# FoX attention without the division by the weights' sum, with the meta block evicted beside the first full block

## The chip, the cores and the metric

One program on one core of a Trainium2 chip. The core has five engines with an in-order queue each: TensorE (PE: matrix products; its weight loads are shown as PEld), VectorE (DVE), ScalarE (ACT), GpSimd (POOL) and SyncE (SP), which starts most transfers. They wait for each other through semaphores. The metric is the time on the device in microseconds (us), the median of several runs.

## The reference

One layer of an encoder trunk over 16 meta tokens and 1024 positions (1040 rows, width 1024), in float32. After a normalisation one projection feeds three mixers: causal pooling, six heads of FoX (softmax attention with a cumulative forget gate as a bias) and six heads of stick-breaking attention. Each head's output is normalised over its 64 channels; an output projection, a gated feed-forward part and a last normalisation follow. What the change touches:

```
def head_rmsnorm(y, gain, n_heads):
    y32 = y.reshape(b, l, n_heads, HEAD_DIM)
    y32 = y32 * lax.rsqrt(jnp.mean(y32 * y32, axis=-1, keepdims=True) + EPS)
    return y32 * gain
...
s = jnp.einsum('bhqd,bhkd->bhqk', qb, k32) * scale
s = s + cb[..., None] - c[:, :, None, :]
s = jnp.where(pos[None, :] <= tq[:, None], s, -jnp.inf)
p = jax.nn.softmax(s, axis=-1)
o = jnp.einsum('bhqk,bhkd->bhqd', p, v)
```

The softmax divides each row by its sum l. With o' = l o the output before that division, o / sqrt(mean(o^2) + EPS) equals o' / sqrt(mean(o'^2) + EPS l^2): the division can be left out if EPS l^2 takes the place of EPS in the head norm.

## The kernel before

Products in full precision are made of halves: a float32 tile is rounded to the PE's format (the high half, ending in h: wh, ph, sh) and the rest (the low half, ending in l) is kept beside it; two or three products replace one. ACT or POOL make the high half (hi_pool is POOL's rounding, L77), DVE or POOL subtract for the low half.

Six pairs of heads go through attention: the first is stick-breaking, then three FoX pairs, then two stick-breaking pairs. The generator `attention` takes, for each pair, blocks of 256 queries (t from 3 to 0) of each head h: `fox_scores` or `sb_scores` make the weights P, a tile of 128 queries by the keys for each half block ii; `weighted`, one block later, turns them (a transpose is a PE product with the identity, L517 and L531), evicts the turned blocks from PSUM as ph (ACT, L520 and L538) and pl (DVE, L521 and L539), three tiles of each in turn, and multiplies them with the values (L511). The meta keys are block 0 with a tile of its own of 256 columns; of the last block of keys only the second half of the queries has weights, so that its pieces are 256 and 128 columns wide. `head_out` adds the two halves of the result (L398, L399). When both heads of a group of 512 queries are done, `head_norm` squares (L404), rounds (L77), subtracts (L408), takes the mean over a head's channels on PE by the matrix hmean (L410, L411), and makes the factor by a logarithm and an exponential on ACT (L413, L414); L415 applies it.

In `fox_scores` DVE adds the bias and finds the maximum (L495), ACT takes the exponential and the sum in one pass (L500), DVE inverts the sum (L501) and multiplies the weights by it (L502):

```
S.activation(P[:, :nk], P[:, :nk], AF.Exp, bias=st[:, 0:1], accum_out=st[:, 1:2])
V.reciprocal(st[:, 2:3], st[:, 1:2])
V.tensor_scalar(P[:, :nk], P[:, :nk], st[:, 2:3], None, ALU.mult)
```

A second generator, the filler, brings work for PE beside attention: the projections of the next pair (L289, with weights split on POOL, L77 and L164), the pooling mixers' pieces (L597 on, mostly DVE additions, L627 to L652), and at the end the output projection (L701). `interleave` writes the two in an order set by estimated costs; a scheduler then orders each engine's queue by a simulated timeline, so that the order of instructions is fixed when the program is built. The feed-forward part (L890, L1075) follows.

Of the kernel before, what the change touches and what calls it, by code (L numbers as in the profile page):

```python
# [17 lines left out]
NM = 16  # L18
# [12 lines left out]
def hymba_trunk(  # L31
# [59 lines left out]
    def mm(tag, shape, bufs):  # L91
        return T(ps, shape, F32, tag, bufs)
# [12 lines left out]
            T(at, [128, 512], F32, tag, n)  # L105


    ident = cst.tile([128, 128], F32, name="ident")
    make_identity(nc, ident)
    identb = cst.tile([128, 128], BF16, name="identb")  # L110
    V.tensor_copy(identb, ident)
    n1 = cst.tile([128, KD], F32, name="n1")
# [285 lines left out]
        S.copy(t[a:a + 64, :n], po[b:b + 64, :])  # L398
        V.tensor_tensor(op[a:a + 64, :], po[a:a + 64, :], t[a:a + 64, :n], ALU.add)  # L399

    def head_norm(op, gi, yt, last=False):
# [8 lines left out]
        PE.matmul(pm, hmean, sh, start=True, stop=False)  # L410
        PE.matmul(pm, hmean, sl, start=False, stop=True)  # L411
        f = T(at, [128, 512], F32, "nt", 2)
        S.activation(f, pm, AF.Ln, bias=epst[:, 0:1])  # L413
# [72 lines left out]

    def fox_scores(pr, h, t, cb):
        pr.pt = []
        for ii in range(2):
# [8 lines left out]
            st = T(ap_, [128, 3], F32, "fs", 4)  # L498
            V.tensor_scalar(st[:, 0:1], mx[:, len(pcs) - 1:len(pcs)], -1.0, None, ALU.mult)
            S.activation(P[:, :nk], P[:, :nk], AF.Exp, bias=st[:, 0:1], accum_out=st[:, 1:2])  # L500
            V.reciprocal(st[:, 2:3], st[:, 1:2])  # L501
            V.tensor_scalar(P[:, :nk], P[:, :nk], st[:, 2:3], None, ALU.mult)  # L502
            pr.pt.append(P)
            yield 1.2 * nk / 512

    def weighted(pr, h, t, ptiles, po):
        nkb = 2 * t + 3

        def av(kb, xs, c, first):
            for ix, x in enumerate(xs):  # L510
                PE.matmul(po[:, c:256], pr.v[h][:, kb, :], x, start=first and ix == 0,  # L511
                          stop=(kb == nkb - 1 and ix == 1), skip_group_check=True)


        tp = mm("s", [128, 512], SB_)
        for ii in range(2):
            PE.transpose(tp[:, 128 * ii:128 * ii + 128], ptiles[ii][:, 0:128], ident)  # L517
        ph = T(ap_, [128, 512], F32R, "ph", 3)
        pl = T(ap_, [128, 512], F32R, "pl", 3)
        S.copy(ph[:, :256], tp[:, :256])  # L520
        V.tensor_tensor(pl[:, :256], tp[:, :256], ph[:, :256], ALU.subtract)  # L521
        av(0, (ph[:, :256], pl[:, :256]), 0, True)
        kbs = list(range(1, nkb))
        for g in range(0, len(kbs), 2):
            pair = kbs[g:g + 2]
            tp = mm("s", [128, 2, 2, 128], SB_)
            for gi, kb in enumerate(pair):
                kc = slice(NM + 128 * (kb - 1), NM + 128 * kb)
                for ii in range(2):
                    if kb <= 2 * t + ii + 1:  # L530
                        PE.transpose(tp[:, gi, ii, :], ptiles[ii][:, kc], ident)  # L531
            ph = T(ap_, [128, 512], F32R, "ph", 3)
            pl = T(ap_, [128, 512], F32R, "pl", 3)
            tpf = tp.rearrange("p a b c -> p (a b c)")

            rngs = [(0, 256), (384, 512)] if pair[1] == nkb - 1 else [(0, 512)]
            for a, b in rngs:
                S.copy(ph[:, a:b], tpf[:, a:b])  # L538
                V.tensor_tensor(pl[:, a:b], tpf[:, a:b], ph[:, a:b], ALU.subtract)  # L539
            for gi, kb in enumerate(pair):  # L540
                c = 128 if kb == nkb - 1 else 0
                av(kb, (ph[:, 256 * gi + c:256 * gi + 256], pl[:, 256 * gi + c:256 * gi + 256]), c, False)
            yield 0.5

    def attention():

# [4 lines left out]
        def back(p, h, t, pts):  # L551
# [4 lines left out]
            head_out(po, h, ops[j][:, 256 * tt:256 * tt + 256])  # L556
            if h == 1 and tt == 0:
                yo = T(at, [128, 512], F32, "nt", 2)
                head_norm(ops[j], c - 2, yo, p == 5 and j == 0)
                if p < 5:  # L560
                    nc.scalar.dma_start(ysd[c][:, 512 * j:512 * j + 512], yo)
                else:
# [617 lines left out]
```

## Time and profile before

| | us |
|---|---|
| median of 3 runs | 1284.89 (1284.74 to 1286.3) |
| the profiled execution | 1286.02 |
| its span, first to last instruction | 1284.2 |
| PE busy | 1215.3 (95%) |
| DVE busy | 947.2 (74%) |
| ACT busy | 630.5 (49%) |
| POOL busy | 480.2 (37%) |
| mean granted PE clock | 0.982 of full speed |

Matrix products overlap in PE, and their ends are modelled, so that a busy PE need not be one at its peak; where its busy time is short of a stretch, it waited. An engine's queue is in order: what stands in front of an instruction delays it even if it has nothing to do with it. The order shown below is that of the built program and has no times; times are the trace's.

### The profile page before, as it was taken

The numbers are of one execution on the slowest core, as the hardware profiler recorded it, in microseconds if no ns is written. First come the engines' busy times: TensorE is split into PE (matmuls) and PEld (weight loads), VectorE is DVE, ScalarE is ACT, GpSimd is POOL, SyncE is SP. The second block draws the span as 40 slices with busy tenths as digits, with TensorE's granted clock in tenths as the row PEclk, the third lists the DMA queues.
The fourth block names the chain that finished last, engine by engine and source line by source line (L and its number), as shares of the span: only waits on it lengthen the run. The fifth ranks groups of instructions, "written<-read, shape, count | busy, mean of one in ns | idle before, by whom it ended". The sixth has DMA issues, their size and how long they took to land.

```text
span 1284.2 us, 18471 instructions
## 1 busy us (share of the span) xinstructions
PE 1215.3 (95%) x6310; PEld 1023.5 (80%) x6310; DVE 947.2 (74%) x1713; ACT 630.5 (49%) x1318; POOL 480.2 (37%) x534
## 2 busy tenths in 40 slices
PE   7699899999898989999898999999999999999997
PEld 5587778888788878778687888888888888788885
DVE  8667886868977779997777676666767656876557
ACT  6456754645448677767743333332223334444443
POOL 6459046362363764550105453443544410000001
PEclk9999899999899989999999999999999999999999
DMA  5100011010100161201505554445544439565653
GB/s 180 40 17 27 13 47 34 26 42 18 50 29 30 38 213 67 74 25 50 197 25 180 171 167 151 138 136 181 189 164 160 136 131 344 172 212 199 197 173 139
DMA packets 73146, 147.13 MB, mean 115 GB/s; under 512 B 9052, under 2 KB 21340, under 8 KB 73052
## 3 DMA queue, kind: packets, MB, share of 16 engines
q1 hardware_dynamic: 69728, 142.01, 33.3%
q10 hardware_dynamic: 3324, 3.95, 0.9%
q8 instruction: 50, 0.82, 0.3%
q14 instruction: 44, 0.36, 0.1%
HBM read 103.98 MB, written 41.94 MB: 114 GB/s over the span
## 4 chain that ended last, share of the span: by engine, by line
PE 66%; DVE 11%; issue 4%; ACT 4%; DMA 2%; POOL 1%; SPq 0%; DVEq 0%; POOLq 0%; ACTq 0%
PE s L890 21%; PE mm L289 10%; PE mm L890 8%; PE s L1075 7%; PE mm L701 4%; PE o L511 4%; PE mm L1075 3%; PE o L1075 3%; PE s L531 3%; DVE r L470 3%; PE s L429 1%; PE s L431 1%; DVE x L703 1%; DVE P L472 1%; DMA raw<-in_w_down 1%
## 5 line engine op out<-in xcount | busy, mean ns | idle before, releaser
L890 PE MATMUL s<-t,wh 128*128 128x512 f32 x544 | 170.4, 392 | 3.5 <-ACT wh L876 3.5
L890 PEld LDWEIGHTS s<-t,wh 128*128 128x128 f32 x544 | 102.7, 189 | 25.7 <-ACT wh L876 4.2
L890 PE MATMUL s<-s,wh 128*128 128x512 f32 x384 | 118.5, 390 | 0.0
L876 ACT CAST wh<-ss 128x512 fp32r<-128x512 f32 x80 | 49.5, 621 | 133.6 <-PE s L890 93.0
L890 PE MATMUL s<-t,wl 128*128 128x512 f32 x272 | 106.3, 391 | 0.0
L289 PE MATMUL mm<-x,wh 128*128 128x512 f32 (+1 forms) x320 | 100.1, 387 | 1.1 <-DVE pt L354 1.1
L538 ACT CAST ph<-s 128x512 fp32r<-128x512 f32 (+2 forms) x168 | 70.7, 434 | 60.0 <-PE s L531 23.9
L890 PE MATMUL mm<-t,wh 128*128 128x512 f32 x320 | 98.5, 389 | 0.0
L1063 ACT CAST wh<-sg 128x512 fp32r<-128x512 f32 x74 | 46.0, 623 | 104.6 <-PE s L1075 46.1
L876 ACT CAST wh<-raw 128x512 fp32r<-128x512 f32 x68 | 41.7, 621 | 111.2 <-PE s L890 72.4
L539 DVE TENSOR_TENSOR pl<-s,ph 128x512 fp32r<-128x512 f32 (+2 forms) x168 | 81.1, 492 | 19.9 <-ACT ph L538 17.5
L1064 DVE TENSOR_TENSOR wl<-sg,wh 128x512 fp32r<-128x512 f32 x74 | 51.0, 690 | 56.9 <-ACT wh L1063 56.6
L511 PE MATMUL o<-pl,v 128*128 128x256 f32 (+1 forms) x288 | 85.8, 314 | 0.7 <-DVE pl L521 0.6
L511 PE MATMUL o<-ph,v 128*128 128x256 f32 (+1 forms) x288 | 80.2, 292 | 3.8 <-ACT ph L520 2.4
L890 PEld LDWEIGHTS s<-s,wh 128*128 128x128 f32 x384 | 71.9, 188 | 14.9
L984 DVE TENSOR_TENSOR cg<-s,tmp 128x512 f32<-128x512 f32 x60 | 41.2, 687 | 56.9 <-PE s L890 56.9
L1114 POOL TENSOR_TENSOR r<-r,mhalf 128x1 f32<-128x1 f32 x8 | 4.4, 547 | 209.0 <-DVE r L1113 207.4
L289 PE MATMUL mm<-xa,wh 128*128 128x264 f32 (+3 forms) x248 | 78.5, 320 | 1.2 <-ACT rbc L239 0.7
L289 PE MATMUL mm<-xa,wl 128*128 128x264 f32 (+3 forms) x248 | 76.5, 313 | 1.2 <-POOL wl L164 1.2
L289 PE MATMUL mm<-xb,wh 128*128 128x264 f32 (+3 forms) x248 | 77.0, 313 | 0.0
L531 PE MATMUL s<-ident,P 128*128 128x128 f32 x432 | 68.8, 278 | 6.3 <-DVE pl L521 3.6
L878 DVE TENSOR_TENSOR wl<-ss,wh 128x512 fp32r<-128x512 f32 x80 | 68.7, 862 | 8.2 <-ACT wh L876 6.8
(287 smaller groups left out, 3636.6 us busy)
## 6 DMA issues: line engine op xcount, KB each, us to landing
sg<-lsd SPq DMA_DIRECT2D x70, 256.0 KB, 3.2
raw<-in_w_gate SPq DMA_DIRECT2D x22, 512.0 KB, 5.4
raw<-in_w_up SPq DMA_DIRECT2D x22, 512.0 KB, 3.9
wr<-in_w_in SPq DMA_DIRECT2D x80, 128.0 KB, 2.2
raw<-in_w_down SPq DMA_DIRECT2D x20, 512.0 KB, 3.6
lsd<-cg SPq DMA_DIRECT2D x40, 256.0 KB, 3.2
raw<-rsd SPq DMA_DIRECT2D x40, 256.0 KB, 3.4
raw<-in_w_down SPq DMA_DIRECT2D x34, 256.0 KB, 3.1
```

The source lines that it names most:

```text
L289: PE.matmul(p[:, :n], w[k][ww], xx(k, t0, n), start=i == 0, stop=i == 23)
L511: PE.matmul(po[:, c:256], pr.v[h][:, kb, :], x, start=first and ix == 0, stop=(kb == nkb - 1 and ix == 1), skip_group_check=True)
L531: PE.transpose(tp[:, gi, ii, :], ptiles[ii][:, kc], ident)
L538: S.copy(ph[:, a:b], tpf[:, a:b])
L539: V.tensor_tensor(pl[:, a:b], tpf[:, a:b], ph[:, a:b], ALU.subtract)
L701: PE.matmul(p, y_[:, ts_], w_[:, ds], start=i == 0, stop=i == 3 * len(ws) - 1)
L876: S.copy(wh, a)
L878: V.tensor_tensor(wl, a, wh, ALU.subtract)
L890: PE.matmul(p, ws[ww][:, k, :], xs_[xx][:, k, :], start=first and i == 0, stop=i == 11, skip_group_check=True)
L1063: S.copy(wh, a)
L1064: V.tensor_tensor(wl, a, wh, ALU.subtract)
L1075: PE.matmul(p, x[xx][:, 128 * b:128 * b + 128], y[yy], start=first and i == 0, stop=last and i == 2, skip_group_check=True)
```

## The change

Four edits:

- The identity is kept as a tile in PE's format (identr), of which ident is another view; it is built in a scratch tile and copied by DVE.
- `fox_scores` leaves out the reciprocal and the multiplication; the exponential's sum goes into a tile lt, one for each 512 queries of a pair, with a column for each of four blocks of 128 queries and each head.
- `head_norm` gets lt for the FoX pairs. DVE makes EPS l^2 (l2, 128x8), POOL spreads it over 64 channels as two halves l2h and l2l (tiles of the rings ph and pl), and eight products with the identity, 128 columns each, turn them into PSUM on top of the mean (L427 of the changed kernel). The logarithm then has no EPS to add.
- `weighted` treats block 0 as any other: blocks go in groups of two from block 0 on, so that the meta block shares an eviction of 512 columns with the first full block, and the last group is the last block's 128 columns alone.

```diff
+    identr = cst.tile([128, 128], F32R, name="identr")
+    ident = identr.bitcast(F32)
+    tmp0 = T(sp_, [128, 128], F32, "c3")
+    make_identity(nc, tmp0)
+    V.tensor_copy(identr, tmp0)
...
+        if lt is not None:
+            l2 = T(ap_, [128, 4, 2], F32, "l2", 2)
+            V.scalar_tensor_tensor(l2, lt, EPS, lt, ALU.mult, ALU.mult)
+            wide = l2.unsqueeze(3).to_broadcast([128, 4, 2, 64])
+            l2h = T(ap_, [128, 512], F32R, "ph", 3).rearrange("p (i h c) -> p i h c", i=4, h=2)
+            hi_pool(l2h, wide)
+            l2l = T(ap_, [128, 512], F32R, "pl", 3).rearrange("p (i h c) -> p i h c", i=4, h=2)
+            G.tensor_tensor(l2l, wide, l2h, ALU.subtract)
+            for i in range(4):
+                for x in (l2h, l2l):
+                    PE.matmul(pm[:, 128 * i:128 * i + 128], x[:, i].rearrange("p a b -> p (a b)"), identr,
+                              start=False, stop=i == 3 and x is l2l, skip_group_check=True)
...
-            S.activation(P[:, :nk], P[:, :nk], AF.Exp, bias=st[:, 0:1], accum_out=st[:, 1:2])
-            V.reciprocal(st[:, 2:3], st[:, 1:2])
-            V.tensor_scalar(P[:, :nk], P[:, :nk], st[:, 2:3], None, ALU.mult)
+            b = 2 * (t % 2) + ii
+            S.activation(P[:, :nk], P[:, :nk], AF.Exp, bias=st[:, 0:1], accum_out=pr.lt[t // 2][:, b, h:h + 1])
...
-        tp = mm("s", [128, 512], SB_)
-        for ii in range(2):
-            PE.transpose(tp[:, 128 * ii:128 * ii + 128], ptiles[ii][:, 0:128], ident)
...
-        S.copy(ph[:, :256], tp[:, :256])
-        V.tensor_tensor(pl[:, :256], tp[:, :256], ph[:, :256], ALU.subtract)
-        av(0, (ph[:, :256], pl[:, :256]), 0, True)
-        kbs = list(range(1, nkb))
...
-            rngs = [(0, 256), (384, 512)] if pair[1] == nkb - 1 else [(0, 512)]
-            for a, b in rngs:
-                S.copy(ph[:, a:b], tpf[:, a:b])
-                V.tensor_tensor(pl[:, a:b], tpf[:, a:b], ph[:, a:b], ALU.subtract)
...
+        for g in range(0, nkb, 2):
+            group = [(kb, ii) for kb in range(g, min(g + 2, nkb)) for ii in range(kb == nkb - 1, 2)]
+            n = 128 * len(group)
+            tp = mm("s", [128, 512], SB_)
+            for i, (kb, ii) in enumerate(group):
+                k0 = NM + 128 * (kb - 1) if kb else 0
+                PE.transpose(tp[:, 128 * i:128 * i + 128], ptiles[ii][:, k0:k0 + 128], ident)
...
+            S.copy(ph[:, :n], tp[:, :n])
+            V.tensor_tensor(pl[:, :n], tp[:, :n], ph[:, :n], ALU.subtract)
...
-                head_norm(ops[j], c - 2, yo, p == 5 and j == 0)
+                head_norm(ops[j], c - 2, yo, p == 5 and j == 0, prs[p].lt[j] if fox else None)
```

Counted over the program, DVE has 137 instructions fewer (48 multiplications, 48 reciprocals and 48 evictions less; six l2 and a copy more), ACT 48 fewer, POOL 12 more, PE 48 more.

DVE's queue of the kernel before, in the third FoX pair, from the subtraction of the head norm (L408) to the eviction of a meta block (L521); e, r and pt are tiles of the pooling mixer, P the weights:

```order
L408 TENSOR_TENSOR nt_4422<-nt_4418,pt_4420 128x512
L502 TENSOR_SCALAR P_4444<-P_4444,fs_4455 128x656
L639 TENSOR_TENSOR e_4396<-e_4394 128x265
L501 RECIPROCAL fs_4486<-fs_4486 128x1
L639 TENSOR_TENSOR e_4398<-e_4396 64x257
L647 SCALAR_TENSOR_TENSOR r_4400<-e_4396,pt_4387 64x256
L502 TENSOR_SCALAR P_4475<-P_4475,fs_4486 128x784
L647 SCALAR_TENSOR_TENSOR r_4400<-e_4398,pt_4387 64x256
L627 TENSOR_TENSOR pt_4491<-mm_4432,rbc_416 128x256
L521 TENSOR_TENSOR pl_4564<-s_4560,ph_4563 128x256
```

The same place in the changed kernel, where L412 is the head norm's subtraction and L548 the merged eviction of 512 columns:

```order
L650 TENSOR_TENSOR e_4322<-e_4320 128x265
L650 TENSOR_TENSOR e_4324<-e_4322 64x257
L658 SCALAR_TENSOR_TENSOR r_4326<-e_4322,pt_4313 64x256
L412 TENSOR_TENSOR nt_4356<-nt_4352,pt_4354 128x512
L658 SCALAR_TENSOR_TENSOR r_4326<-e_4324,pt_4313 64x256
L638 TENSOR_TENSOR pt_4435<-mm_4380,rbc_418 128x256
L548 TENSOR_TENSOR pl_4510<-s_4504,ph_4509 128x512
```

The multiplications and reciprocals are gone, and two of the mixer's additions (L639 before, L650 now) and one of its L647 (L658 now) have moved ahead of the head norm's subtraction, so that two mixer instructions stand between it and the eviction instead of eight others.

PE's queue at the same head norm before (L411 the mean's second product, L531 transposes, L612 to L614 the pooling mixer, L511 the value products):

```order
L411 MATMUL o_4424<-nt_4422,hmean 128x512
L531 MATMUL s_4569<-ident,P_4260 128x128
L531 MATMUL s_4569<-ident,P_4291 128x128
L613 MATMUL mm_4407<-r_4329,pwh_4151 128x264
L614 MATMUL mm_4407<-r_4327,pwl_4153 128x264
L511 MATMUL o_4559<-ph_4563,v_3745 128x256
L531 MATMUL s_4623<-ident,P_4260 128x128
L531 MATMUL s_4623<-ident,P_4291 128x128 x2
L511 MATMUL o_4559<-pl_4564,v_3745 128x256
L612 MATMUL mm_4509<-r_4403,pwh_4151 128x256
```

And in the changed kernel (L415 the mean's second product, L427 the new products, L533 the value products):

```order
L415 MATMUL o_4358<-nt_4356,hmean 128x512
L427 MATMUL o_4358<-identr,ph_4363 128x128
L427 MATMUL o_4358<-identr,pl_4365 128x128
L427 MATMUL o_4358<-identr,ph_4363 128x128
L427 MATMUL o_4358<-identr,pl_4365 128x128
L427 MATMUL o_4358<-identr,ph_4363 128x128
L427 MATMUL o_4358<-identr,pl_4365 128x128
L427 MATMUL o_4358<-identr,ph_4363 128x128
L427 MATMUL o_4358<-identr,pl_4365 128x128
L533 MATMUL o_4503<-ph_4509,v_3691 128x256
L544 MATMUL s_4587<-identr,P_4229 128x128
L533 MATMUL o_4503<-pl_4510,v_3691 128x256
```

The eight new products stand in one piece behind the mean's, ahead of the next block's value products. POOL's queue around the last two FoX head norms, before (pt_4078 and pt_4420 are their rounded squares, r and last tiles of the mixer, L74 zeroes a tile of queries):

```order
L77 TENSOR_SCALAR pt_4078<-nt_4076 128x512
L630 COPY last_4223<-pt_4221 128x16
L626 COPY pt_4311<-last_4223 128x16
L630 COPY last_4314<-pt_4311 128x16
L626 COPY pt_4387<-last_4314 128x16
L77 TENSOR_SCALAR r_4236<-r_4233 128x248
L74 MEMSET q_1182_4879 64x512
L74 MEMSET v_5085 128x128
L630 COPY last_4390<-pt_4387 128x16
L77 TENSOR_SCALAR r_4327<-r_4324 128x264
L77 TENSOR_SCALAR pt_4420<-nt_4418 128x512
```

And in the changed kernel, where ph_4017 with pl_4019 and ph_4363 with pl_4365 are the spread halves of l2, and pt_4008 is the first of the two rounded squares:

```order
L77 TENSOR_SCALAR ph_4017<-l_973_4015 128x512
L424 TENSOR_TENSOR pl_4019<-l_973_4015,ph_4017 128x512
L77 TENSOR_SCALAR pt_4008<-nt_4006 128x512
L641 COPY last_4161<-pt_4159 128x16
L637 COPY pt_4247<-last_4161 128x16
L641 COPY last_4250<-pt_4247 128x16
L637 COPY pt_4313<-last_4250 128x16
L77 TENSOR_SCALAR r_4174<-r_4171 128x248
L77 TENSOR_SCALAR ph_4363<-l_1077_4361 128x512
L424 TENSOR_TENSOR pl_4365<-l_1077_4361,ph_4363 128x512
```

POOL makes both halves of l2 (the rows ph and L424) ahead of the rounded square that the mean needs: at the first of the two norms directly ahead of it, at the second eight rows ahead (its square, pt_4354, stands eight rows below the last one shown).

## Rows read from the trace of the kernel before

**Rows 1.** Engine table of the page: busy us (share of the span) and instructions.

```profile
PE 1215.3 (95%) x6310; PEld 1023.5 (80%) x6310; DVE 947.2 (74%) x1713; ACT 630.5 (49%) x1318; POOL 480.2 (37%) x534
```

**Rows 2.** Busy by stretch: length, PE, PEld, DVE, ACT, POOL, clock, DMA, GB/s.

```profile
160.00:176.00 16.00, 13.38 (x79) 10.84 (x78) 15.69 (x43) 9.38 (x23) 7.83 (x14) 0.92 0.22 67
176.00:192.00 16.00, 15.35 (x110) 14.00 (x109) 12.28 (x38) 8.45 (x19) 6.78 (x12) 0.97 0.08 27
192.00:318.00 126.00, 125.56 (x856) 113.11 (x855) 96.00 (x294) 68.41 (x174) 60.95 (x93) 1.00 0.10 30
318.00:345.00 27.00, 20.45 (x128) 17.64 (x126) 25.74 (x70) 12.58 (x27) 10.31 (x17) 0.87 0.13 45
345.00:392.00 47.00, 46.84 (x319) 42.35 (x320) 36.52 (x106) 25.03 (x63) 25.22 (x38) 1.00 0.10 32
392.00:640.00 248.00, 230.70 (x1286) 191.60 (x1285) 203.06 (x360) 184.52 (x429) 109.98 (x125) 0.98 0.26 89
```

**Rows 3.** Waits of PE, 160 to 392 us: total, times, longest.

```profile
PE s L531 <- DVE pl L521: 3.6, 1, 3.6
```

**Rows 4.** DVE's timeline: start, us, engine, line, operation, tiles, shapes.

```profile
331.31 0.55 DVE L639 TENSOR_TENSOR e<-e 128x269 f32<-128x269 f32 x1
...
332.93 0.69 DVE L502 TENSOR_SCALAR P<-P,fs 128x656 f32<-128x656 f32 x1
333.55 0.96 DVE L639 TENSOR_TENSOR e<-e 128x265 f32<-128x265 f32 x1
...
335.83 0.61 DVE L502 TENSOR_SCALAR P<-P,fs 128x784 f32<-128x784 f32 x1
...
337.35 0.41 DVE L521 TENSOR_TENSOR pl<-s,ph 128x256 fp32r<-128x256 f32 x1
```

**Rows 5.** Busy time by stretch, as rows 2.

```profile
336.00:344.00 8.00, 6.18 (x27) 5.61 (x28) 7.84 (x20) 1.86 (x4) 1.85 (x3) 0.59 0.20 66
```

**Rows 6.** Line L502 alone by stretch: length, DVE busy (instructions), clock, DMA.

```profile
160.00:176.00 16.00, 0.69 (x1) 0.92 0.22 67
176.00:192.00 16.00, 2.59 (x4) 0.97 0.08 27
...
318.00:345.00 27.00, 2.90 (x4) 0.87 0.13 45
...
sum 1220.00, DVE 30.22; mean DVE 3.78
```

**Rows 7.** Groups by shape, 60 to 640 us: busy, mean ns | idle before.

```profile
L501 DVE RECIPROCAL fs<-fs 128x1 f32<-128x1 f32 x48 | 7.6, 159 | 7.3 <-ACT P L500 6.7
```

**Rows 8.** The same view, evictions of weighted.

```profile
L539 DVE TENSOR_TENSOR pl<-s,ph 128x512 fp32r<-128x512 f32 x72 | 48.5, 684 | 14.4 <-ACT ph L538 13.9
...
L538 ACT CAST ph<-s 128x512 fp32r<-128x512 f32 x72 | 40.7, 587 | 30.4 <-PE s L531 19.2 <-PE o L511 8.2 <-DVE pl L521 2.2
...
L539 DVE TENSOR_TENSOR pl<-s,ph 128x256 fp32r<-128x256 f32 x48 | 20.0, 416 | 4.0 <-ACT ph L538 2.3 <-PE o L511 1.4
L521 DVE TENSOR_TENSOR pl<-s,ph 128x256 fp32r<-128x256 f32 x48 | 19.8, 413 | 3.4 <-ACT ph L520 2.9 <-PE o L511 0.2
...
L520 ACT CAST ph<-s 128x256 fp32r<-128x256 f32 x48 | 17.7, 368 | 14.2 <-PE s L517 11.8 <-PE o L511 1.8
```

**Rows 9.** PE's timeline, two places.

```profile
151.47 1.03 PE L531 MATMUL s<-ident,P 128*128 128x128 f32 x8
152.26 0.36 PE L511 MATMUL o<-pl,v 128*128 128x256 f32 x1
...
209.68 0.27 PE L511 MATMUL o<-pl,v 128*128 128x128 f32 x1
209.79 0.44 PE L289 MATMUL mm<-x,wh 128*128 128x512 f32 x1
```

**Rows 10.** POOL's groups by shape, 160 to 392 us.

```profile
L312 POOL TENSOR_TENSOR q<-pt,q 64x512 fp32r<-64x512 f32 x6 | 8.4, 1413 | 0.3
...
L77 POOL TENSOR_SCALAR pt<-nt 128x512 fp32r<-128x512 f32 x6 | 4.3, 709 | 17.8 <-ACT nt L404 17.8
```

More of the change, by code (lines that the diff above doesn't have):

```diff
@@ L105, in hymba_trunk @@
             T(at, [128, 512], F32, tag, n)
-    ident = cst.tile([128, 128], F32, name="ident")
-    make_identity(nc, ident)
+    identr = cst.tile([128, 128], F32R, name="identr")
[3 more added lines that the diff above has]
+    V.tensor_copy(identr, tmp0)
     identb = cst.tile([128, 128], BF16, name="identb")
@@ L399, in head_out, with head_norm @@
         V.tensor_tensor(op[a:a + 64, :], po[a:a + 64, :], t[a:a + 64, :n], ALU.add)
-    def head_norm(op, gi, yt, last=False):
+    def head_norm(op, gi, yt, last=False, lt=None):
         hi = S.copy if last else hi_pool
@@ L409, in head_norm @@
         pm = mm("o", [128, 512], OB)
-        PE.matmul(pm, hmean, sh, start=True, stop=False)
-        PE.matmul(pm, hmean, sl, start=False, stop=True)
+        PE.matmul(pm, hmean, sh, start=True, stop=False, skip_group_check=True)
+        PE.matmul(pm, hmean, sl, start=False, stop=lt is None, skip_group_check=True)
+        if lt is not None:
[10 more added lines that the diff above has]
+                              start=False, stop=i == 3 and x is l2l, skip_group_check=True)
         f = T(at, [128, 512], F32, "nt", 2)
-        S.activation(f, pm, AF.Ln, bias=epst[:, 0:1])
+        if lt is None:
+            S.activation(f, pm, AF.Ln, bias=epst[:, 0:1])
+        else:
+            S.activation(f, pm, AF.Ln)
         S.activation(f, f, AF.Exp, scale=-0.5)
@@ L488, in fox_scores @@
         pr.pt = []
+        if (h, t) == (0, 3):
+            pr.lt = [T(ap_, [128, 4, 2], F32, "lt", 4) for _ in range(2)]
         for ii in range(2):
@@ L497, in fox_scores @@
                                        mx[:, pc:pc + 1])
-            st = T(ap_, [128, 3], F32, "fs", 4)
-            V.tensor_scalar(st[:, 0:1], mx[:, len(pcs) - 1:len(pcs)], -1.0, None, ALU.mult)
-            S.activation(P[:, :nk], P[:, :nk], AF.Exp, bias=st[:, 0:1], accum_out=st[:, 1:2])
-            V.reciprocal(st[:, 2:3], st[:, 1:2])
-            V.tensor_scalar(P[:, :nk], P[:, :nk], st[:, 2:3], None, ALU.mult)
+            st = T(ap_, [128, 1], F32, "fs", 4)
+            V.tensor_scalar(st, mx[:, len(pcs) - 1:len(pcs)], -1.0, None, ALU.mult)
+            b = 2 * (t % 2) + ii
+            S.activation(P[:, :nk], P[:, :nk], AF.Exp, bias=st[:, 0:1], accum_out=pr.lt[t // 2][:, b, h:h + 1])
             pr.pt.append(P)
@@ L512, in av @@
                           stop=(kb == nkb - 1 and ix == 1), skip_group_check=True)
-        tp = mm("s", [128, 512], SB_)
-        for ii in range(2):
-            PE.transpose(tp[:, 128 * ii:128 * ii + 128], ptiles[ii][:, 0:128], ident)
-        ph = T(ap_, [128, 512], F32R, "ph", 3)
-        pl = T(ap_, [128, 512], F32R, "pl", 3)
-        S.copy(ph[:, :256], tp[:, :256])
-        V.tensor_tensor(pl[:, :256], tp[:, :256], ph[:, :256], ALU.subtract)
-        av(0, (ph[:, :256], pl[:, :256]), 0, True)
-        kbs = list(range(1, nkb))
[L524 to L531, printed above, removed]
+        for g in range(0, nkb, 2):
[5 more added lines that the diff above has]
+                PE.transpose(tp[:, 128 * i:128 * i + 128], ptiles[ii][:, k0:k0 + 128], ident)
             ph = T(ap_, [128, 512], F32R, "ph", 3)
             pl = T(ap_, [128, 512], F32R, "pl", 3)
-            tpf = tp.rearrange("p a b c -> p (a b c)")
-            rngs = [(0, 256), (384, 512)] if pair[1] == nkb - 1 else [(0, 512)]
-            for a, b in rngs:
-                S.copy(ph[:, a:b], tpf[:, a:b])
-                V.tensor_tensor(pl[:, a:b], tpf[:, a:b], ph[:, a:b], ALU.subtract)
-            for gi, kb in enumerate(pair):
+            S.copy(ph[:, :n], tp[:, :n])
+            V.tensor_tensor(pl[:, :n], tp[:, :n], ph[:, :n], ALU.subtract)
+            for kb in range(g, min(g + 2, nkb)):
                 c = 128 if kb == nkb - 1 else 0
-                av(kb, (ph[:, 256 * gi + c:256 * gi + 256], pl[:, 256 * gi + c:256 * gi + 256]), c, False)
-            yield 0.5
+                a = 256 * (kb - g)
+                av(kb, (ph[:, a:a + 256 - c], pl[:, a:a + 256 - c]), c, kb == 0)
+            if kb < nkb - 1:
+                yield 0.5
     def attention():
```

## The prediction

> **What bounds the kernel now.** I read four views, from coarse to fine. The engine table of the page first: TensorE (PE) is busy 1215.3 of 1284.2 us, VectorE (DVE) 947.2, ScalarE (ACT) and GpSimd (POOL) far less [rows 1]. So a microsecond taken from DVE counts only where PE stands still for DVE. Then busy time by stretch, since the edit lies in attention: the three FoX pairs run from about 160 to 392 us beside the projections, the stick-breaking pairs before and after [rows 2]. In 192 to 318 and 345 to 392 PE is busy for all but 0.44 and 0.16 us; DVE has 30.00 and 10.48 us to spare there. These stretches are PE's. In 318 to 345 it is the other way: DVE works 25.74 of 27 us, PE only 20.45, and PE's granted clock is 0.87. Likewise in 160 to 176: DVE 15.69 of 16, PE 13.38. These two hold a pooling mixer's piece (L627 to L652), all DVE work, beside FoX's own. Third, the waits: the longest one of PE in the FoX pairs is 3.6 us, for the DVE half of the meta block's eviction (L521) [rows 3]. Last, DVE's timeline before the end of that wait: between L408 and L521 the in-order queue holds two normalising passes (L502, 0.69 and 0.61 us) and mixer work [rows 4]. After this wait the granted clock over 336 to 344 is 0.59 [rows 5]: much of it at the lower of the two levels, 1.2 GHz.
>
> **What goes from DVE.** 48 passes L502 (30.22 us) and 48 reciprocals L501 (7.62 us, 0.159 each) [rows 6, 7]. Of the passes, 0.69 us lie in 160 to 176, 2.59 in 176 to 192, 2.90 in 318 to 345; the rest lies almost all in PE's stretches. With them goes the step from the exponential over DVE to the transposes.
>
> **What is merged.** Each of the 48 calls of weighted (24 FoX, 24 stick-breaking) evicted a meta block of 256 columns and, at its end, pieces of 256 and 128; now only pieces of 512 and one of 128. Two pieces of 256 become one of 512. DVE: 0.413 + 0.416 - 0.684 = 0.145 us saved a call; ACT: 2 x 0.368 - 0.587 = 0.149 us [rows 8]. Over 48 calls that is 7.0 and 7.2 us. The transposes and the products with the values keep their number and their columns.
>
> **What is added.** Six head norms (the FoX ones) get one tiny DVE instruction, a rounding and a subtraction of 128x512 on POOL, and eight PE products of 128 columns. The scale l2 needs only the sums, which are there long before; in the order POOL makes both halves ahead of the rounding of the square (sh) that the norm needs anyway.
>
> The terms, against the profiled execution (1286.02 us; its span of 1284.2 and 1.82 around it), with minus for a gain:
>
> A, 318 to 345. DVE sheds 2.90 + 4 x 0.159 + 3 x 0.145 = 4.0 us (four passes with their reciprocals [rows 6, 7]; 24 FoX calls in 232 us make some 3 merges in 27), and DVE is what the stretch waits for, so it shortens by about that. The clock of 0.59 over 8 us costs PE 3.3 us of full speed [rows 5]; most is hidden while DVE bounds, and I take 1.0 back. A = -5.0. Bounds: 0 (the next wait takes over) and -10.1 (all 6.55 us of PE's idle time and 0.13 x 27 = 3.5 us of clock).
>
> B, 160 to 192. DVE sheds 0.69 + 2.59 + 5 x 0.159 + 3 x 0.145 = 4.5 us, but only some 1.1 us of it in the full first half. PE's idle time is 2.62 + 0.65 = 3.3 us, the clock's share 0.08 x 16 + 0.03 x 16 = 1.8. I take -2.0, bounds 0 and -5.1.
>
> C, the rest of the FoX pairs. DVE sheds the other passes and reciprocals, 30.22 - 6.18 = 24.0 and 39 x 0.159 = 6.2 us, and some 18 merges, 2.6, beside PE's work, which hides them: PE's idle time there is 0.6 us [rows 2]. A short wait can hide in a matmul's modelled tail: a 128-column product lasts 0.27 us in the trace while the next one starts after 0.11 [rows 9], so up to 0.16 us at each of the 24 hand-offs that go. Bounds 0 and -(0.6 + 3.8) = -4.4; I take -1.0, near the idle time.
>
> D, stick-breaking pairs. 24 merges are worth 3.5 us of DVE and 3.6 of ACT. In 392 to 640 PE is idle for 17.3 us, with DVE busy for 82% and ACT for 74% [rows 2], so neither alone is the bound. I take half of DVE's part, -1.7; bounds 0 and -7.1 (both in a chain).
>
> E, the new products. No row shows them. Nearest: eight 128-column transposes, each with weights of its own, take 152.26 - 151.47 = 0.79 us, 0.099 each [rows 9]. 48 x 0.099 = 4.8 us, all on PE, which is the bound; one head norm of the six lies where PE has idle time, so I take 4.4. Bounds: 4.0 (that one free) and 48 x 0.27 = 13.0 (each alone). The Trainium skill, in "TensorE: Matmul & The Clock Gate", section "Back-to-back issue gap", gives about 81 ns for a 128-column product in a stream of weight loads and products; by that the 48 would cost 3.9 us and the sum would come out 0.9 us lower. The trace's 0.099 does not reach it.
>
> F, POOL. 6 x (0.709 + 1.413) = 12.7 us by its like on the same shape or half the partitions [rows 10]. POOL has the time (60.95 of 126 us busy in 192 to 318), but DVE may slow beside it: the same mixer addition took 0.55 us at 331.31 and 0.96 at 333.55 [rows 4]. 12.7 us of POOL cover some 14 instructions of 0.9 us at most, 14 x 0.41 = 5.7 us of DVE; a quarter of that lies where DVE is the bound. Bounds 0 and 1.4; I take 0.5. The Trainium skill ("GPSIMD Engine Reference", section "8. Key points") says why: GpSimd and VectorE share their way into SBUF, and vector instructions with two SBUF inputs contend for it. The pair of rows fits that, and shows no more; by the rule alone, all new POOL work would slow its neighbours, and F would stand at its upper bound.
>
> Costed at nothing: the copy of the identity at the start (DVE makes it, and on POOL the order has one instruction fewer ahead of PE's first weights, not more); ACT's logarithm without a bias, which only drops an operand; the DVE square of the sums, six instructions as small as L501's 0.159 us, hidden beside PE and worth 1 us if that cover were gone.
>
> Sum: -5.0 - 2.0 - 1.0 - 1.7 + 4.4 + 0.5 = -4.8. The profiled execution would go to 1281.2; it lies 1.13 us over the median of the runs, 1284.89, so for the median **1280.1 us**. What is late next: PE itself, in the order of the projections.
>
> **Rivals.**
>
> 1. All of PE's waiting between 160 and 345 goes, since the chain from the exponential to the transposes loses two DVE steps, and the clock stays up: -(6.55 + 3.27) - (3.5 + 1.8) = -15.1; with C and D as above and E and F against it, -15.1 - 2.7 + 4.9 = -12.9, **1272 us**. For it: the wait of 3.6 us has two of the passes right ahead of it. Against: in these stretches the mixer's DVE work remains, and DVE was 95% to 98% busy.
>
> 2. Slower: the sum's square becomes the wait. PE takes its products in order, with scores, transposes and value products of the other blocks behind the eight new ones. If POOL's two instructions are late, behind weight splits or behind a memset that itself waits for PE, the head norm and all behind it stand; and while the l2 tile holds one of the three ph/pl sets, the evictions have two. Each time costs 0.709 + 1.413 = 2.1 us: six are 12.7 us, and 12.7 - 9.7 + 4.9 = +7.9, **1293 us**. It decides from 1.2 us a head norm on: six of them take back the net gain of 4.8 us and the 2.6 that a measurement needs. Against: the order puts POOL's l2 work ahead of sh in every one of the six.
>
> 3. No change: DVE's time is hidden nearly everywhere; only A comes, -5.0, and E and F take it back: **1284.8 us**. For it: 173 of 232 us in the FoX pairs need PE for all but 0.6 us. Against: the stretch A is real, and so is D.
>
> **Chances.** Forecast 0.43; rival 1 0.20; rival 2 0.17; rival 3 0.20. About 0.2%, 2.6 us, is what a measurement here can tell from none. Faster: forecast and rival 1, 0.63; same: 0.20; slower: 0.17. The scheduler also reorders everything after the edit by a few instructions, of which I cannot price the sign. Range: the sums of the better bounds of A, B and half of C and D reach -15.2 - 5.8 + 4.9 = -16, 1268; upward rival 2 with five of its six waits, 10.6 - 4.8 = +5.8, 1290. The forecast's own range is 1275 to 1284.
>
> **What would show it.** A: no wait of PE over 1 us for a merged eviction where the mixer's pieces lie, PE's clock there over 0.9, and DVE's busy time down by about 44 us in all (30.2 + 7.6 + 7.0 less about 1). E: 48 products under a new line, some 0.1 us apart, with no wait for POOL in front; a wait there speaks for rival 2. C is wrong if the full stretches shorten by over 4 us. The forecast fails if PE's idle time from 160 to 392 us, 10.4 us [rows 2], does not fall by at least 4, or if new waits on ACT's evictions come up next to the six head norms.

## The result and the profile after

The changed kernel takes 1274.99 us (median of 4 runs, 1274.24 to 1275.25), the kernel before 1285.34 beside it: ratio 0.9914, 95% interval 0.9902 to 0.9926. By the ratio the gain is 11.0 us (9.5 to 12.6), by the two medians 10.4. The forecast was a gain of 4.8, to 1280.1.

The engine table of the page after, to be held against [rows 1] (busy time, share of the span, instructions):

```profile
span 1273.5 us, 18419 instructions
...
PE 1214.7 (95%) x6358; PEld 1024.5 (80%) x6358; DVE 916.6 (72%) x1576; ACT 623.6 (49%) x1270; POOL 486.5 (38%) x546
```

PE's busy time hardly moves (1215.3 to 1214.7), although 48 products came in; its idle time falls from 68.9 to 58.8 us. The mean granted clock goes from 0.982 to 0.987. DVE's busy time falls by 30.6 us, not by the 44 forecast.

The stretches of [rows 2] in the changed kernel (length, then busy time of PE, PEld, DVE, ACT, POOL; clock, DMA share, GB/s):

```profile
160.00:176.00 16.00, 13.96 (x93) 12.28 (x92) 13.68 (x40) 8.38 (x18) 6.57 (x13) 0.91 0.22 67
176.00:192.00 16.00, 16.00 (x115) 14.73 (x115) 9.67 (x28) 8.39 (x21) 8.83 (x15) 1.00 0.11 36
192.00:318.00 126.00, 125.44 (x857) 112.76 (x855) 80.20 (x227) 65.60 (x154) 61.39 (x95) 1.00 0.09 29
318.00:345.00 27.00, 24.07 (x170) 21.83 (x169) 25.78 (x68) 14.71 (x34) 10.77 (x19) 0.94 0.17 55
345.00:392.00 47.00, 46.89 (x315) 41.90 (x313) 26.77 (x72) 22.61 (x52) 26.88 (x41) 1.00 0.08 26
392.00:640.00 248.00, 234.42 (x1311) 195.49 (x1312) 201.42 (x343) 180.83 (x411) 111.01 (x126) 0.99 0.26 90
```

By most of its own signs the forecast holds (the 44 us of DVE are the one that fails): in 318 to 345 PE is busy 24.07 us instead of 20.45, at a clock of 0.94 instead of 0.87; PE's idle time from 160 to 392 falls from 10.4 to 5.6 us, and the wait of 3.6 us [rows 3] is gone, the longest for a merged eviction being 0.7:

```profile
engine line waited for: us in total, times, longest us
PE s L544 <- DVE mx L517: 2.1, 4, 0.9
PE s L449 <- DVE pl L548: 1.2, 3, 0.7
PE s L449 <- DVE mx L517: 1.1, 1, 1.1
PE s L503 <- ACT cb L504: 0.5, 1, 0.5
```

But fixed times say little when everything behind an edit shifts. The next two fences cut both executions at the same products instead: PE's first FoX bias product, the products of the projections at 387.0 (384.1 after), the output projection's start, and two products of the feed-forward. First before, then after:

```profile
0.00:161.10 161.10, 133.49 (x770) 113.78 (x770) 124.36 (x219) 96.90 (x209) 87.40 (x118) 0.95 0.18 55
161.10:387.00 225.90, 215.76 (x1437) 192.62 (x1438) 180.76 (x532) 119.36 (x291) 107.82 (x169) 0.98 0.11 35
387.00:474.80 87.80, 80.06 (x492) 69.03 (x490) 62.51 (x122) 66.81 (x169) 53.65 (x70) 0.96 0.24 84
474.80:647.80 173.00, 163.44 (x878) 134.01 (x877) 146.91 (x255) 122.05 (x272) 59.60 (x60) 0.99 0.26 88
647.80:725.40 77.60, 74.06 (x323) 60.46 (x322) 61.67 (x65) 30.57 (x45) 27.48 (x18) 0.98 0.37 122
725.40:1284.20 558.80, 548.50 (x2419) 453.62 (x2417) 370.99 (x524) 194.79 (x335) 144.26 (x100) 1.00 0.53 176
```

```profile
0.00:157.50 157.50, 130.40 (x770) 111.09 (x770) 125.08 (x213) 96.94 (x203) 87.39 (x118) 0.97 0.18 57
157.50:384.10 226.60, 220.60 (x1489) 197.78 (x1490) 153.10 (x429) 117.19 (x272) 109.83 (x178) 0.98 0.11 35
384.10:466.00 81.90, 75.44 (x476) 66.14 (x475) 57.16 (x101) 60.09 (x152) 57.69 (x73) 0.98 0.26 88
466.00:639.70 173.70, 166.47 (x895) 136.34 (x896) 149.45 (x250) 125.12 (x270) 59.69 (x60) 0.99 0.26 87
639.70:712.50 72.80, 71.20 (x313) 58.16 (x312) 59.90 (x63) 29.07 (x43) 27.57 (x18) 1.00 0.40 129
712.50:1273.50 561.00, 550.54 (x2421) 455.02 (x2419) 371.93 (x525) 195.19 (x336) 144.35 (x100) 0.99 0.53 175
```

The FoX stretch, where the forecast put A, B, C, E and F (-3.1 together), is 0.7 us longer: DVE loses 27.7 us of busy time there, PE's idle time falls by 4.1, and the products fill it. Most of the gain lies elsewhere: -3.6 before any FoX, -5.9 in 387 to 475, -4.8 at the feed-forward's start, and +2.2 behind it.

These sizes depend on the cut, since the orders move products across its edges: 387 to 475 holds 492 products before and 476 after, the stretch behind it 878 and 895, the feed-forward's start 323 and 313. Cut after equal amounts of PE work (the columns of the products in both traces, without the 48 new ones), the six stretches change by -3.6, -1.4, -2.5, -1.0, -4.0 and +1.8 us. By either cut FoX gives less than the forecast had there, and the gains of the first and the fifth stretch stand by both.

The new products as a group, and the first four of one head norm's eight on PE's timeline (start, duration):

```profile
L427 PE MATMUL o<-identr,ph x24: 220/274/307, 242.3 to 423.1; 128*128 128x128 f32 x24
L427 PE MATMUL o<-identr,pl x24: 221/276/278, 242.3 to 423.2; 128*128 128x128 f32 x24
```

```profile
241.96 0.48 PE L415 MATMUL o<-nt,hmean 128*128 128x512 f32 x1
242.27 0.22 PE L427 MATMUL o<-identr,ph 128*128 128x128 f32 x1
242.33 0.28 PE L427 MATMUL o<-identr,pl 128*128 128x128 f32 x1
242.44 0.27 PE L427 MATMUL o<-identr,ph 128*128 128x128 f32 x1
242.55 0.28 PE L427 MATMUL o<-identr,pl 128*128 128x128 f32 x1
```

Where two of them are neighbours (36 pairs) they start 0.11 us apart in the median and 0.099 on the mean. The first stand right behind the mean's last product, and PE waits for nothing in front of any of the 48; from 160 to 430 us it waits nowhere for POOL. Rival 2 is out.

### The profile page after: what moved, and what is told of

Read it like the earlier page. It is cut to its first block, busy times and chain, and to the rows that moved or that the text cites. A ratio compares the mean times of both kernels' runs of the same rounds, so it can differ in the third digit from the quotient of the medians.

```text
span 1273.5 us, 18419 instructions
## 1 busy us (share of the span) xinstructions
PE 1214.7 (95%) x6358; PEld 1024.5 (80%) x6358; DVE 916.6 (72%) x1576; ACT 623.6 (49%) x1270; POOL 486.5 (38%) x546
## 4 chain that ended last, share of the span: by engine, by line
PE 70%; DVE 15%; issue 5%; ACT 5%; DMA 3%; POOL 1%; DVEq 0%; SPq 0%; POOLq 0%; ACTq 0%
PE s L901 22%; PE mm L292 12%; PE mm L901 8%; PE s L1086 7%; PE mm L712 4%; PE o L533 4%; DVE r L490 3%; PE s L544 3%; PE o L1086 3%; PE mm L1086 3%; DVE P L492 1%; PE s L449 1%; PE s L451 1%; DVE pl L548 1%; DVE x L714 1%
## 5 line engine op out<-in xcount | busy, mean ns | idle before, releaser
L548 DVE TENSOR_TENSOR pl<-s,ph 128x512 fp32r<-128x512 f32 (+1 forms) x168 | 92.3, 569 | 36.3 <-ACT ph L547 32.2
L547 ACT CAST ph<-s 128x512 fp32r<-128x512 f32 (+1 forms) x168 | 79.2, 495 | 60.2 <-PE o L533 32.7
L544 PE MATMUL s<-identr,P 128*128 128x128 f32 x528 | 81.7, 275 | 6.3 <-DVE pl L548 2.3
L533 PE MATMUL o<-pl,v 128*128 128x256 f32 (+1 forms) x288 | 81.6, 308 | 0.6 <-DVE pl L548 0.6
L533 PE MATMUL o<-ph,v 128*128 128x256 f32 (+1 forms) x288 | 76.9, 283 | 0.1
L544 PEld LDWEIGHTS s<-identr,P 128*128 128x128 f32 x528 | 62.0, 140 | 16.8 <-DVE pl L548 4.5
```

The lines of the kernel that those rows point to most:

```text
L544: PE.transpose(tp[:, 128 * i:128 * i + 128], ptiles[ii][:, k0:k0 + 128], ident)
L547: S.copy(ph[:, :n], tp[:, :n])
L548: V.tensor_tensor(pl[:, :n], tp[:, :n], ph[:, :n], ALU.subtract)
```

## The experiments

Two theories at first: W, the work taken out is the gain; O, the scheduler's other order behind the edit is. Ratios are to runs of the kernel before on the same chip, with the 95% interval; 0.001 is 1.29 us.

**Each half of the edit, the squares, and order alone.**

merge_only has the changed `weighted` in the kernel before; nonorm_only has everything but that. no_l2 and identr_only:

```diff
-                head_norm(ops[j], c - 2, yo, p == 5 and j == 0, prs[p].lt[j] if fox else None)
+                head_norm(ops[j], c - 2, yo, p == 5 and j == 0, None)
```
```diff
-    make_identity(nc, ident)
+    make_identity(nc, tmp0)
+    V.tensor_copy(identr, tmp0)
```

> The kernel before with the merged weighted() alone; the weights are still divided by their sum. Theory W (work: the merge and the lighter DVE each take away PE's short waits of 1 to 4 us, and the lower clock behind each): the first stick-breaking pair's gain (3.6 us by 161 us) comes here whole, the FoX stretches little, so about -5 us against before, 1280. Theory O (order: the scheduler lays all instructions after the edit in another order, and the gain outside FoX is that order's): the size has no reason, between -3 and +3, and the gain by 161 us need not come. Theory M (the merge is nearly all of it, on ACT as much as on DVE): -8 or more, 1277.

Measured: 1.0014 (1.0000 to 1.0027).

> The changed kernel with the weighted() of before: no division by the sum, square of the sum in the head norm, but the meta block evicted by itself. Theory W: FoX's DVE load falls by 37.8 us, of which only the stretch 318 to 345 and 160 to 192 pay; with the 48 products against it about -4 us, 1281, and merge_only and this together come near -10.5. Theory M: -2 or less, since FoX's DVE time is hidden. Theory O: no sum rule; the two differ from -10.5 together by over 4 us.

Measured: 1.0031 (1.0020 to 1.0042).

> The changed kernel with the head norm of before: the square of the sum is left out (six small DVE instructions, twelve of POOL, 48 products of PE), so the term epsilon times the square is not computed right. By the prediction's terms E and F this is 4.9 us under the changed kernel, 1270. Rival (the products fall where PE would wait for DVE or ACT anyway, or are hidden under POOL): under 2 us, 1273 to 1275.

Measured: 0.9924 (0.9907 to 0.9941): no gain over the changed kernel's 0.9914.

> The kernel before with only the identity's tile made as in the changed kernel: no work is taken out, but the scheduler lays out the instructions in another order from there on (some 16% of PE's instructions stand elsewhere). Theory W: within 1.5 us of before. Theory O: 3 us or more away, to either side; if it is -3 or better, with the gain at 120 to 136 us, the order and not the edit made a good part of the 11 us.

Measured: 0.9980 (0.9969 to 0.9991).

Neither half gains by itself, together they gain 11 us: W, which adds, is wrong as put, and so is M. identr_only adds a copy and takes nothing out, and moves by 2.6 us, so one order says little. The next runs hold the order, or vary it.

**The order held.** A first trace gives each engine's order; the second trace, with the changed work, gets ordering edges without semaphores (NoSync) between neighbours:

```diff
+                    for a, b in zip(seq, seq[1:]):
+                        tc.add_manual_dep(t[b], t[a].name, mybir.DependencyInfo(
+                            mybir.DependencyClass.NoSync, mybir.DependencyReason.DATA), reason="pinned order")
```

(The lines of such kernels have other numbers: L537 is L531 before, L527 is L521, L500 is L495.) In before_order_nonorm the second trace loses

```diff
-            V.reciprocal(st[:, 2:3], st[:, 1:2])
-            V.tensor_scalar(P[:, :nk], P[:, :nk], st[:, 2:3], None, ALU.mult)
```

> The kernel before with the order of the four engines held instruction by instruction as it was (ordering edges without semaphores), and only the 48 multiplications and 48 reciprocals left out, so the weights are not normalised. 37.8 us of DVE go, nothing else changes. Theory W (work): the prediction's A + B + C come, -8 against before, 1278. Theory O (the gain of 11 us is the new order, the work that went was hidden): -3 to 0, 1283 to 1286.

Measured: 0.9987 (0.9977 to 0.9998), 1.7 us (0.3 to 3.0). O's value. Its engine table, and the stretch 318 to 345 with PE's waits there:

```profile
PE 1216.4 (95%) x6310; PEld 1023.0 (80%) x6310; DVE 917.6 (71%) x1617; ACT 630.2 (49%) x1318; POOL 474.6 (37%) x534
```

```profile
318.00:345.00 27.00, 22.37 (x140) 19.08 (x139) 24.34 (x69) 12.96 (x29) 9.29 (x19) 0.87 0.13 45
336.00:344.00 8.00, 6.95 (x30) 5.87 (x30) 6.63 (x17) 2.23 (x6) 1.62 (x4) 0.60 0.21 69
```

```profile
PE mm L618 <- POOL r L82: 1.4, 2, 0.7
PE s L537 <- DVE pl L527: 1.1, 1, 1.1
PE s L537 <- DVE mx L500: 0.6, 1, 0.6
```

The wait of 3.6 us shrinks to 1.1, POOL's part of the mixer is late next, and the clock over 336 to 344 is 0.60, as it was [rows 5]. The same projection products that start at 324.7 and 353.9 us before lie 1.8 us closer together here; that is all of A. Even of this a part may be scatter. In before_tail_of_after (below), which has the order and the work of before up to 610 us, the wait is 3.6 us again, yet the same two products lie 1.1 us closer together than before, with a higher granted clock behind the wait:

```profile
336.00:344.00 8.00, 5.92 (x34) 5.16 (x35) 7.84 (x20) 2.51 (x6) 1.66 (x3) 0.79 0.21 69
```

after_order_norm_back and after_order_both_back go the other way, from the changed kernel's order, in which the added instructions (EXTRA) take a place that the scheduler finds:

```diff
+                EXTRA.append(V.reciprocal(rc, pr.lt[t // 2][:, b, h:h + 1]).ins)
+                EXTRA.append(V.tensor_scalar(P[:, :nk], P[:, :nk], rc, None, ALU.mult).ins)
...
+            cuts = ((0, 256), (256, n)) if MOD[0] and g == 0 else ((0, n),)
```

> The changed kernel with its order held, and the 48 reciprocals and multiplications put back into DVE's queue as extra instructions (the weights are normalised and the head norm then adds a wrong square). Theory W: +8 against the changed kernel, 1283. Theory O: +0 to +3, 1275 to 1278.

Measured: 0.9971 (0.9960 to 0.9982), 7.3 us over the changed kernel (5.2 to 9.4 by the two intervals): W's value.

> As the one before, and the first eviction of each call of weighted cut into two of 256 columns as well, so that ACT and DVE have all the work back that the change took from them, in the changed kernel's order. Theory W: all of the 11 us and the products' 4.4 on top, +10 to +15, 1285 to 1290. Theory O: under +4, 1279 at most.

Measured: 1.0118 (1.0099 to 1.0136), 26 us over it, beyond both theories. This one says little of the merge: the added second halves stand later in ACT's and DVE's queues than the first ones, and PE waits for them:

```profile
PE o L542 <- DVE pl L558: 9.9, 11, 2.0
```

So the same division costs 1.7 us in the old order and 7.3 in the new one. Order and work belong together. A likely reason, argued and not shown: the new order was laid out by a simulated timeline in which DVE hands over sooner, so that PE stands still where the old work is put into it. What the merge is worth with the order of before held was not run.

> The changed kernel with its order held and only the 48 products of the sum's square left out (POOL still makes the halves; epsilon times the square is missing). The prediction's term E: -4.4, 1270.6. If they fall into time in which PE would wait anyway: under -2, 1273 or more. no_l2, in an order of its own, showed no gain over the changed kernel.

Measured: 0.9905 (0.9891 to 0.9920), 1.2 us under the changed kernel and within the uncertainty of it. PE's busy time:

```profile
PE 1208.8 (95%) x6310; PEld 1017.0 (80%) x6310; DVE 917.5 (72%) x1576; ACT 622.9 (49%) x1270; POOL 485.8 (38%) x546
```

5.9 us less than with the products (0.12 each), but PE's idle time is 3.8 us longer (62.6 for 58.8). Term E was right as busy time and too dear as time.

**Other orders of each kernel.** The hand-set pacing is moved by a hair; this leaves the work and lays from some 8% to over 20% of PE's instructions elsewhere.

```diff
-    SBC, FOXC = 65.0, 38.0
+    SBC, FOXC = 65.5, 38.0
```

(other order 1; 65.0, 38.3 in other order 2.)

> The changed kernel, with one number of the hand-set pacing moved by a hair (the stick-breaking pairs' nominal cost 65.0 to 65.5), so that the same work is laid out in another order (about 8% of PE's instructions stand elsewhere). Theory J (joint: the lighter work lets the scheduler find an order with fewer waits, and nearly any such order has them): within 3 us of the changed kernel, 1272 to 1278. Theory L (luck of one order): 1280 or more, as the two half edits came out.

> As after_other_order_1, with the FoX pairs' nominal cost moved from 38.0 to 38.3 instead (about 20% of PE's instructions stand elsewhere). Theory J: 1272 to 1278. Theory L: 1280 or more.

> The kernel before with 65.0 moved to 65.5 (13% of PE's instructions elsewhere), no work changed. Theory J: within 3 us of before, 1283 to 1289. Theory L: as wide as the after-orders, so that some order of the old work comes down to 1280 or less.

> The kernel before with 38.0 moved to 38.3 (13% of PE's instructions elsewhere). Theory J: 1283 to 1289. Theory L: some order of the old work comes down to 1280 or less, or goes up as far.

> merge_only in the first other order (65.0 to 65.5). Theory J2 (each part is worth something on the mean over orders, merge some 3 us, no normalisation some 3, together the 6 to 8 that three orders of both gave): the mean of the three orders of merge_only comes out near -3 us against before, so this one near 1279 to 1284. Theory P (the parts pay only together: the scheduler needs the wait of PE behind exponential, multiplication and eviction gone whole): the mean stays at 0, this one 1284 to 1290.

> merge_only in the second other order (38.0 to 38.3). As before: J2 1279 to 1285, P 1284 to 1292.

> nonorm_only in the first other order. J2: 1280 to 1286, mean of the three near -3. P: 1284 to 1292, mean 0 or above (the 48 products cost some 1 to 4 us).

> nonorm_only in the second other order. J2: 1280 to 1287. P: 1284 to 1294.

Measured, with the runs in the kernels' own orders:

```
order      before                  merge alone             no division alone       both
own        1                       1.0014 (1.0000-1.0027)  1.0031 (1.0020-1.0042)  0.9914 (0.9902-0.9926)
other 1    0.9990 (0.9978-1.0001)  0.9984 (0.9971-0.9997)  1.0037 (1.0024-1.0050)  0.9952 (0.9935-0.9970)
other 2    1.0025 (1.0015-1.0035)  0.9959 (0.9943-0.9974)  1.0022 (1.0012-1.0031)  0.9957 (0.9943-0.9971)
mean       1.0005                  0.9986                  1.0030                  0.9941
```

On the mean of three orders both edits gain 0.0064, 8.2 us; the two other orders of the changed kernel gain 6.2 and 5.5 against before as it was, so 3 to 5 of the 11 us are the one order's luck and 6 to 8 the edit's. Each theory is half right: the changed kernel's other orders took 1281.0 and 1281.6 us, as L has it, but no order of the old work came below a median of 1283.4 (identr_only), as J has it. The merge alone gains 2.4 us on the mean, which is within the scatter of its three orders (0.9959 to 1.0014); the division alone costs 3.2 (1.0022 to 1.0037). The halves do not add up, as P has it: the sum of their means is +0.8 us, both together -8.2, and no order of both reaches one of the old work (0.9957 against identr_only's 0.9980 at the nearest). Why they pay only together is not shown; P's reason, a wait that has to go whole, was not tested.

Where that is, from one profiled execution of each: time between the starts of the same PE products, minus that of before (163.4, 648 and 725 us before):

```
run                     to 163   163-648   648-725   725-end
before, other 1           +4.2      -6.0      -0.2      +2.2
before, other 2           -0.6      +2.6       0.0      +0.2
merge, own                -4.6      +6.3      +1.1      +2.3
merge, other 1            -0.2      -5.7      +0.3      +0.8
merge, other 2            -6.1      +0.2      -4.9      +4.6
no division, own          +1.3      -1.5      +0.4      +2.4
no division, other 1      +4.7      -3.9      +1.7      +1.5
no division, other 2      -0.2      +3.4      -0.5      +0.8
both, own                 -4.7      -3.5      -4.8      +2.2
both, other 1             +0.9      -6.4      -4.9      +4.8
both, other 2             -4.1      +1.0      -3.9      +0.4
```

Order by order, the merge shortens the first column by 4.4 to 5.5 us with the division and by 3.8 to 6.0 without: six pairs of six. The mark at 163.4 is a FoX bias product that the orders place differently among the others; taken at the 770th product instead (161.1 us before), the six pairs give 2.8 to 4.9 us. A second execution of merge_only's order (merge_tail_of_after, the same up to 611 us) has -2.2 in the first column for -4.6, so an execution adds some 2 us of scatter. The middle, with all of FoX, scatters by 13 us and shows no family; within it, from 368 to 480 us, the other orders of before gain some 5 and 9 and the changed kernel 7, and so does every other order that was run, by 4 to 15, whatever its work: before's own order stands badly there. In 648 to 725 all three orders of both gain 3.9 to 4.9, one of the merge alone 4.9, those of before and of no division none.

The first column's gain, in merge_only: two windows and then PE's longest waits of 112 to 160 us, first before, then merge_only (one of 0.7 us for another tile left out).

```profile
128.00:144.00 16.00, 14.67 (x90) 13.25 (x91) 14.62 (x32) 12.35 (x31) 2.18 (x6) 0.79 0.07 20
144.00:160.00 16.00, 13.69 (x94) 12.56 (x95) 14.00 (x31) 11.42 (x31) 1.32 (x3) 0.89 0.03 9
```

```profile
PE s L517 <- DVE P L472: 1.5, 1, 1.5
PE mm L612 <- POOL r L77: 1.0, 1, 1.0
PE s L429 <- DVE pl L539: 0.9, 2, 0.5
```

```profile
128.00:144.00 16.00, 14.36 (x107) 12.69 (x108) 14.36 (x31) 12.81 (x31) 2.82 (x7) 1.00 0.08 20
144.00:160.00 16.00, 11.88 (x87) 10.35 (x86) 14.76 (x32) 12.00 (x32) 3.77 (x7) 1.00 0.03 9
```

```profile
PE mm L601 <- POOL r L77: 2.2, 2, 1.3
PE s L522 <- DVE P L472: 1.0, 2, 0.7
PE s L522 <- DVE pl L526: 0.7, 1, 0.7
```

Before, the clock is 0.79 and 0.89; with the merge the longest wait for attention is 0.7 us, one for POOL's part of the mixer 1.3 us, and the clock is 1.00. It is tempting to put the gain down to the clock: 0.21 x 16 + 0.11 x 16 = 5.1 us of full speed. A second execution of before's order (before_tail_of_after) speaks against it:

```profile
128.00:144.00 16.00, 14.07 (x94) 12.38 (x94) 14.98 (x34) 12.19 (x31) 2.34 (x6) 0.89 0.07 20
144.00:160.00 16.00, 13.68 (x95) 12.29 (x94) 14.19 (x33) 11.76 (x31) 1.33 (x3) 0.89 0.03 9
```

Its clock over 128 to 144 is 0.89, which is 1.6 us of full speed more than in before, yet the product that starts at 144 us before starts only 0.3 us earlier: PE waits 1.4 us for DVE there instead of 0.8. With DVE busy for 14.6 to 15.0 of 16 us, part of the lower clock lies in time in which PE would wait. And in merge_tail_of_after, with the merge in the order of merge_only, the clock over 144 to 160 is 0.89 too:

```profile
144.00:160.00 16.00, 12.17 (x85) 11.22 (x84) 13.12 (x29) 10.81 (x29) 2.06 (x3) 0.89 0.03 9
```

So the merge's gain in the first pair is shown; how much of it is DVE's and ACT's shorter work and how much the clock is not.

**The feed-forward's start.** Is its gain the new order after attention, with no regard to the work? Only what is traced behind attention is held in the changed kernel's order; 47 of PE's instructions move, mainly transposes of token blocks (L744 before) that go ahead of feed-forward products. hymba_changed is the changed kernel's program, hymba_trunk that of before, or of merge_only.

```diff
+    order = build(hymba_changed, None)[2]
+    nc, arrays, got = build(hymba_trunk, order)
```

> The kernel before, no work changed. Only what is traced after attention (output blocks' transposes, feed-forward) keeps on PE, DVE, ACT and POOL the relative order that it has in the changed kernel: 47 of PE's instructions move, above all transposes of token blocks (L744) that go ahead of feed-forward products. Theory T (the 4.5 us that all orders of the changed kernel gain between 650 and 725 us is this order and nothing of the edit's work): -4.5 against before, 1282. Rival U (the early transposes pay only when attention leaves PE, DVE or ACT free earlier, so it is the lighter work after all): within 1.5 us of before.

Measured: 0.9998 (0.9984 to 1.0012).

> merge_only with the same order after attention. merge_only itself was 1.0014 of before in its own order. Theory T: 4.5 us less, 1.0014 - 0.0035 = 0.998, 1284. Rival U: 1.0014, 1288.

Measured: 0.9997 (0.9978 to 1.0016), against 1.0014.

The medians say U. The profiled executions say T: 648 to 725 us shortens by 4.6 us and by 4.6 to 5.1. PE's wait there before, after, and in before_tail_of_after:

```profile
PE s L890 <- ACT wh L876: 3.5, 1, 3.5
```

```profile
PE s L901 <- ACT wh L887: 1.6, 1, 1.6
```

```profile
PE s L896 <- ACT wh L882: 1.5, 1, 1.5
```

In these two kernels single executions lie 10 and 13 us apart (1281.6 to 1291.1, 1281.3 to 1294.6), and the profiled one of the first was its fastest. So the order moves the wait, but whether the 4.6 us are there in every execution, and what takes them back in the median, stays open.

## Why the prediction was wrong

The direction came true, and so did most of the signs; the sum did not, and its parts less than the sum. Too much was priced where the forecast looked, too little or nothing elsewhere, and that the errors left the right direction is in part luck.

- **A, B, C (-8.0): the step that failed.** It took DVE's time as PE's wherever DVE was busy for 95%, and priced that time in the order of before. With this order held, all 48 multiplications and reciprocals are worth 1.7 us (before_order_nonorm; A, B and C also count some 24 merges): A 1.8 in the profile, B and C nothing that shows. A's bound of 0, "the next wait takes over", was nearly the case: POOL's and a rest of the same wait came next. The 1.0 us of clock counted as regained did not come back in that execution. With the changed kernel's order held the same work costs 7.3 us, near the -8.0: the price belongs to the order and not to the work alone.
- **D (-1.7): too small, and in the wrong place.** It counted saved eviction time and looked for it in 392 to 640; no row before 160 us had been read, where the first stick-breaking pair runs. There the merge gives some 3 to 6 us in all six pairs of orders. Part of it is given back later: merge alone gains 2.4 on the mean.
- **E (+4.4): right as busy time (5.9), some 1.2 as time (at most 3.6 by the two intervals).** More of PE's idle time swallowed the rest. From start to start the products are 0.099 us apart on the mean, the row's value [rows 9]. The Trainium skill ("TensorE: Matmul & The Clock Gate", section "Back-to-back issue gap") gives about 81 ns for a 128-column product in a stream of weight loads and products; this trace does not reach it. As an estimate by that figure, 48 products cost 3.9 us and the sum would come out 0.5 us lower than with the 4.4 taken, not 0.9 as the prediction says.
- **F (+0.5)** was not tested apart; no wait for POOL arose, and no_l2, which leaves out E and F, is no faster than the changed kernel.
- **No term at all** stood for what the scheduler does behind the edit, though the text named it: -5.9 in 387 to 475 (-2.5 by equal work), where every other order gains as well, and -4.8 (-4.0) at the feed-forward's start. By the spread of the orders the sum should have had some 5 us to either side for it.
- Rivals: 1 (clock stays up, 1272) is nearest in time, but its place, 160 to 345, is not where the gain lies. 2 is out, and so is 3 in all three orders of the changed kernel.

The books of the profiled executions: PE's idle time -10.1 (68.9 to 58.8), PE's busy time -0.6, together the span's -10.7. The products add 5.9 to the busy time, so 6.5 left it; the granted clock alone would give as much, 0.018 x 1284.2 = 23.1 to 0.013 x 1273.5 = 16.6. That is the most that the clock can be worth, since a slower product in front of a wait costs nothing: among the executions of the kernel before that ran beside the experiments, the 7 with a clock of 0.984 have a median span of 1283.7 us and the 15 with 0.979 one of 1285.9, 2.2 us for 6.4 of full speed (a loose relation: spans at one and the same clock differ by as much).

## What to carry to other kernels

Where a scheduler lays out the queues from a simulated timeline, an edit's time is that of its order too: hold the order with edges to price the work, and move a pacing number by a hair two or three times to price the order, before believing a gain of under 1%. A busy share of 95% does not make an engine the bound: look for what is second in line behind the same wait. Read the stretches that the edit touches from the first one on, not only those where most of the work goes. Before a gain is put down to the clock, take a second execution of the same order: the clock differs between the two, and the time need not follow it.

## What the runs showed of the hardware

- TensorE's granted clock behind the same wait differs between executions. Over 336 to 344 us it was 0.59 after a wait of 3.6 us (before), 0.79 after the same wait in the same order (before_tail_of_after), and 0.60 after one of 1.1 us (before_order_nonorm). A wait of 1.3 us at 146 us in merge_only left it at 1.00 over 144 to 160.
- VectorE's instructions overlap in the records: in [rows 4] one ends at 333.62 (332.93 and 0.69) and the next starts at 333.55. The 48 multiplications and reciprocals sum to 37.8 us [rows 6, 7]; their removal lowers DVE's busy time by 29.6 (947.2 to 917.6), and in merge_only the merge's 7.0 us lower it by 3.4 (to 943.8). So 44 us were forecast for the whole edit and 30.6 came.
- Executions of one kernel spread with the clock: in merge_only from 1284.6 us at a mean granted clock of 0.991 to 1294.1 at 0.978.
